# Expert blocks combined on TensorE: the last three of each layer instead of one, and VectorE-only adds of the rows read back

## The chip, the cores and the metric

The kernel runs on one core of a Trainium2 chip. The metric is the device time of one execution in microseconds. Before the change it is 2536.22 us, the median of three runs (2533.2 to 2540.05).

## The reference, cut to what matters

The program is one hybrid block followed by two decoder layers on 512 tokens of 1024 features. The change touches the mixture of experts that ends each decoder layer. Each token is given two of 32 experts; the reference sorts the 1024 assignments by expert, pads each expert's rows to blocks of 128, and computes

```
def expert_block(args):
    xe, e = args
    hid = jax.nn.silu(xe @ w_gate[e]) * (xe @ w_up[e])
    return hid @ w_down[e]

yb = lax.map(expert_block, (xb, block_expert)).reshape(-1, d)
y_assign = jnp.zeros((n_assign, d), yb.dtype).at[order].set(yb[slot])
y = jnp.einsum('tkd,tk->td', y_assign.reshape(n_tok, TOP_K, d), weights)
...
x = _layernorm(alpha * x + ffn, ln2_g[l], ln2_b[l])
```

Expert width is 256. What must come out is, for each token, the weighted sum of its two experts' rows, added to alpha times the residual and layer-normalised.

## The kernel before, in words

The residual `xr` stays on chip as four tiles of 128 tokens. In `layer_moe` (L1543 on) every layer does 18 blocks of 128 rows (`NB = 18`). Blocks 0 to 3 are one expert each; blocks 4 to 17 hold two experts each, a frequent one in rows 0 to 95 and a rare one in rows 96 to 127, whose numbers SyncE reads from a table at run time (`who_is`, L1832). An overflow path behind `tc.If(rv > 0)` (L1864 to L1916) serves rows that fit in no block.

For each block the loop (L1843 to L1862) issues the next block's weights on SyncE's queue (`load`, L1560 to L1579: for each expert 2 MB of gate and up and 1 MB of down), gathers the token rows of a later block with an indirect DMA on GpSimd's queue, and then calls

- `up` (L1765): 64 products on TensorE into a PSUM tile `gb`, SiLU on ScalarE, and a scale-and-multiply by the routing weight on VectorE into `es`, or `el` for the last block;
- `down` of the block before (L1774): two transposes, a copy to `hT` on ScalarE (L1780), 32 products into two PSUM tiles `db` (L1784);
- `scatter` of the block before (L1788): ScalarE and VectorE copy one half each to a tile `ey` (two buffers), and an indirect DMA on GpSimd's queue writes the rows into `yd` in DRAM, one place for each token and choice.

After the loop come, in program order: the readback of `yd` (`readback`, L1823: eight DMAs on SyncE's queue into four buffers `B`, each held until all scatters have landed); the load of the overflow count by every engine and the branch on it; the eight adds of the readback into `xr` (L1920), for each token tile one on VectorE and one on GpSimd; then `down`, `keep` and `combine` of block 17, whose rows go through no DRAM. `keep` (L1799) splits the block's output into a rounded part `y[:, 0]` (ScalarE) and the rest `y[:, 1]` (VectorE, L1802), and builds a 0/1 matrix `ST` from the token numbers. `combine` (L1807) multiplies `ST` with both parts on TensorE, for each token tile and half (two products, L1812), and VectorE adds the result to `xr`: fused with the sum that the layer norm needs if an `ln` is given (L1817), as a plain add otherwise (L1815, used only in the overflow path). The layer norm follows tile by tile.

The order of the work on each engine is set by a scheduler that simulates the program: an engine takes what is ready, earlier program text first. It doesn't move work across the branch. Buffers are named by pool: `big` has eight buffers `B`, `xH` and `xL` one each (seen as `XW` in the profile; they hold the gate and up weights of block 16), `wraw` has three buffers `R`, PSUM has two `gb`, three `db`, two `xb` and one `hb`.

Of the kernel before, what the change touches and what calls it, by code (L numbers as in the profile page):

```python
# [17 lines left out]
D = 1024  # L18
# [7 lines left out]
ALPHA = 4.0 ** 0.25  # L26
NP = (1, 1, 0, 0)
NS = 4
CAP = 96


# [1511 lines left out]
def layer_moe(k, l):  # L1543
# [37 lines left out]
    with ExitStack() as es:  # L1581
# [214 lines left out]
            tc.add_to_no_dep_group(f"rows{l}", n.ins)  # L1796
            puts.append(n.ins.name)

        def keep(pd, t0, t1, y, ST):  # L1799
            for h in range(2):  # L1800
                A.copy(y[:, 0, h], pd[h])
                V.tensor_sub(y[:, 1, h], pd[h], y[:, 0, h])  # L1802
            V.tensor_scalar(ST[:, 0:256], it, t0, None, op0=OP.is_equal)
            V.tensor_scalar(ST[:, 256:512], it, t1, None, op0=OP.is_equal)
            return ST, y

        def combine(ST, y, ln=None):  # L1807
            for t in range(4):
                for h in range(2):
                    p = gb()  # L1810
                    for b in range(2):
                        mm(p, ST[:, 128 * t:128 * t + 128], y[:, b, h], start=b == 0, stop=b == 1)  # L1812
                    x = xr[:, t, 512 * h:512 * h + 512]
                    if ln is None:
                        V.tensor_add(x, x, p)  # L1815
                    else:
                        V.scalar_tensor_tensor(x, x, 0.0, p, op0=OP.add, op1=OP.add, accum_out=ln.sums(t, h))  # L1817
                if ln:
                    ln.finish(t)
                    if l == 1:  # L1820
                        nc.sync.dma_start(k.out[128 * t:128 * t + 128], xr[:, t])

        def readback(t):  # L1823
            ya = k.big([2, D])
            for j in range(2):
                n = nc.sync.dma_start(ya[:, j], yd[T * j + 128 * t:T * j + 128 * t + 128])
                for put in puts:
                    tc.add_manual_dep(n.ins, put, mybir.DependencyInfo(mybir.DependencyClass.Sync, mybir.DependencyReason.DATA),
                                      reason="rows of every expert")
            return ya  # L1830
# [5 lines left out]
        def weights(b):  # L1836
            if b < NS:
                return [W[b] if b < 2 else load(b)]
            return [load(who_is(idi[0:1, b - NS, j:j + 1])) for j in range(2)]

        later, xT = None, [turned(xg[0])]
        ws = weights(0)
        for b in range(NB):  # L1843
            nxt = weights(b + 1) if b + 1 < NB else None
            if b == NB - 1:
                lgb = k.big([2, D])
                nc.sync.dma_start(lgb[:, 0], k.row(f"ln2_g{l}", 0, D))
                nc.sync.dma_start(lgb[:, 1], k.row(f"ln2_b{l}", 0, D))
            if b + 3 < NB:
                gather(xg[b % 3], xi[:, b + 3:b + 4])  # L1850
            h = up(ws, xT.pop(), tw[:, b:b + 1], rt([256], "el") if b == NB - 1 else half([256], "L", "es"))
            if later:
                pd = [db(), db()]
                down(later[1], later[0], pd)
                scatter(pd, b - 1)
            if b + 1 < NB:
                xT.append(turned(xg[(b + 1) % 3]))
            later = h, ws
            ws = nxt
            if 2 <= b < 6:  # L1860
                with tc.issue_after(k.gone.ins):
                    V.tensor_scalar(xr[:, b - 2], xr[:, b - 2], ALPHA, None, op0=OP.mult)  # L1862
        back = [readback(t) for t in range(4)]
        rv = nc.values_load(nx[0:1, 0:1], min_val=0, max_val=40)  # L1864
        with tc.If(rv > 0):
            turn, oh, o2, c1 = rt([1], "turn"), rt([32], "oh"), rt([32], "o2"), rt([8], "c1")
# [9 lines left out]
            with tc.For_i(0, rv, 1):  # L1876

                pr, r0, r1, tk, wa, t0_, t1_, zz = (c1[:, n:n + 1] for n in range(8))
                V.tensor_scalar(oh, cx, turn, None, op0=OP.is_le)
                V.reduce_sum(pr, oh, axis=AX)  # L1880
                V.tensor_scalar(oh, it[:, 0:32], pr, None, op0=OP.is_equal)
                V.tensor_tensor(o2, cx, ex, op=OP.subtract)
                V.tensor_tensor(o2, o2, oh, op=OP.mult)
                V.reduce_sum(r0, o2, axis=AX)
                V.tensor_sub(r0, turn, r0)
                pick(r1, cap)
                V.scalar_tensor_tensor(r0, r0, 128.0, r1, op0=OP.mult, op1=OP.add)
                V.tensor_copy(ci, pr)
                V.tensor_scalar(turn, turn, 1.0, None, op0=OP.add)
                for j in range(2):  # L1890
                    V.tensor_tensor(se, M[j], all4(oh), op=OP.mult)
                    V.reduce_sum(in_[j], se, axis=AX)
                    V.tensor_tensor(se, se, off, op=OP.mult)
                    V.reduce_sum(wx[j], se, axis=AX)
                    V.tensor_scalar(wx[j], wx[j], r0, None, op0=OP.subtract)
                    V.tensor_scalar(bad, wx[j], 0.0, None, op0=OP.is_lt)
                    V.tensor_sub(bad, bad, in_[j])
                    V.tensor_scalar(bad, bad, 1.0, 1000.0, op0=OP.add, op1=OP.mult)
                    V.tensor_add(wx[j], wx[j], bad)
                q = table()  # L1900
                pick(tk, q[:, 0:32])
                pick(wa, q[:, 32:64])
                tokens(tk, zz, t0_, t1_, None, gi)
                gather(xg[0], gi)
                pe = bass.ds(who_is(ci[0:1, 0:1]), 1)
                g, dn = weg[pe].rearrange("o p n -> (o p) n"), wed[pe].rearrange("o p n -> (o p) n")
                wu = []
                for u in range(2):
                    wu.append(k.big([4, 512]))
                    nc.sync.dma_start(wu[u], g[:, 2048 * u:2048 * u + 2048])  # L1910
                wd = k.wraw.tile([128, 4, 512], F32, name="R")
                nc.sync.dma_start(wd, dn)
                h = up([(wu, wd)], turned(xg[0]), wa, half([256], "L", "es"))
                pd2 = [db(), db()]
                down([(wu, wd)], h, pd2)
                combine(*keep(pd2, t0_, t1_, k.big([2, 2, 512], F32R), half([512], "H", "ST", F32R)))  # L1916

        for t in range(4):
            for j in range(2):
                (G if j else V).tensor_add(xr[:, t], xr[:, t], back[t][:, j])  # L1920
        pd = [db(), db()]
        down(later[1], later[0], pd)
        kept = keep(pd, t0[:, NB - 1:NB], t1[:, NB - 1:NB], k.big([2, 2, 512], F32R), half([512], "H", "ST", F32R))
        ln = LN(k, [lgb[:, 0, :512], lgb[:, 0, 512:]], [lgb[:, 1, :512], lgb[:, 1, 512:]], (1, 1, 1, 1), k.wsp.tile([128, 512], F32, name="ljunk", tag="H"))

        combine(*kept, ln)
# [44 lines left out]
```

## Time and profile before

| | us |
|---|---|
| median of 3 runs | 2536.22 |
| lowest, highest | 2533.2, 2540.05 |
| the profiled execution | 2534.45 |
| its span | 2532.7 |
| mean granted TensorE clock | 0.947 |

The profile holds one execution. All times in it count from the span's start. Its page says how long each engine was busy; the views used below group instructions by line (`L1920` is line 1920), give them in order of time, or sum up what each engine did in a stretch. "Idle before" is the time that an engine stood still ahead of an instruction, and the arrow names what ended it. Expert stages are the stretches in which the page's DMA row is at 9: layer 0's ends near 1620 us, layer 1's near 2481 us.

### The profile page before, as it was taken

The page shows a single profiled execution, that of the slowest core. Times are in us where ns is not written, and L with a number is a line of the kernel's source. Part 1 is how long each engine was busy: PE and PEld are TensorE (multiplying, and loading weights), DVE is VectorE, ACT ScalarE, POOL GpSimd, SP SyncE. Part 2 cuts the span into 40 slices and gives each one's busy share as a digit, 9 for nine tenths or more (in the row PEclk, how much of TensorE's full clock was granted, in tenths as well). Part 3 has the DMA queues.
Part 4 walks back from the last instruction along what each step waited for, and adds up shares of the span by engine and source line. Part 5 has one row for each costly group of instructions (what it writes and reads, how often), then busy time and mean ns, then how long its engine had stood idle before and what let it go on. Part 6 is the DMA issues. An engine that isn't in the chain of part 4 may idle for free. (4 is left out here: it accounts for less than half of the span.)

```text
span 2532.7 us, 33575 instructions
## 1 busy us (share of the span) xinstructions
PE 2291.8 (90%) x12992; PEld 1614.5 (64%) x12992; DVE 1170.5 (46%) x2412; ACT 810.1 (32%) x1670; POOL 518.1 (20%) x490
## 2 busy tenths in 40 slices
PE   6999899999999999999995988778999999788884
PEld 4888577888887777777783322267777677743221
DVE  3762677322336963454475211279444545721105
ACT  4373246333333343333331111144433333211112
POOL 2012342110101322012222210233110232211103
PEclk7999999999999999999997999889999999889997
DMA  6114522222234222121254999921222125369994
GB/s 247 67 53 145 186 84 84 84 99 93 100 109 177 98 75 84 50 84 60 85 205 162 360 405 402 376 76 67 75 71 74 44 75 208 110 239 403 398 410 192
DMA packets 71509, 406.12 MB, mean 160 GB/s; under 512 B 13561, under 2 KB 14233, under 8 KB 30256
## 3 DMA queue, kind: packets, MB, share of 16 engines
q1 hardware_dynamic: 55104, 368.09, 38.1%
q0 software_dynamic: 14032, 30.29, 3.6%
q10 hardware_dynamic: 2208, 5.54, 0.6%
q8 instruction: 104, 1.70, 0.3%
q14 instruction: 61, 0.50, 0.1%
HBM read 390.66 MB, written 32.51 MB: 167 GB/s over the span
## 5 line engine op out<-in xcount | busy, mean ns | idle before, releaser
L233 DVE TENSOR_TENSOR L<-R,H 128x512 fp32r<-128x512 f32 x417 | 302.3, 731 | 432.2 <-ACT H L232 424.9
L238 PE MATMUL bk<-xH,H 128*128 128x512 f32 (+2 forms) x1144 | 450.0, 396 | 1.9 <-DVE h L435 0.9
L239 PE MATMUL bk<-xL,H 128*128 128x512 f32 (+2 forms) x1144 | 451.7, 395 | 0.0
L240 PE MATMUL bk<-xH,L 128*128 128x512 f32 (+2 forms) x1144 | 448.2, 395 | 0.3 <-DVE L L233 0.3
L232 ACT CAST H<-R 128x512 fp32r<-128x512 f32 x447 | 274.1, 620 | 368.8 <-PE bk L239 265.1
L1770 PE MATMUL gb<-B,xT 128*32 128x512 f32 (+1 forms) x1152 | 229.9, 653 | 24.4 <-DMA B<-in_weg_dram 24.4
L240 PEld LDWEIGHTS bk<-xH,L 128*128 128x128 f32 (+1 forms) x1144 | 214.9, 188 | 52.4 <-issue 3.1
L239 PEld LDWEIGHTS bk<-xL,H 128*128 128x128 f32 (+1 forms) x1144 | 215.0, 188 | 47.6 <-issue 2.4
L238 PEld LDWEIGHTS bk<-xH,H 128*128 128x128 f32 (+1 forms) x1144 | 214.1, 188 | 48.6 <-PE bk L428 1.3
L239 PE MATMUL bk<-L,xH 128*128 128x256 f32 x640 | 184.1, 289 | 13.4 <-DVE L L233 13.4
L238 PE MATMUL bk<-H,xH 128*128 128x256 f32 x640 | 184.7, 290 | 3.8 <-ACT xH L1479 1.4
L240 PE MATMUL bk<-H,xL 128*128 128x256 f32 x640 | 181.9, 289 | 4.3 <-DVE xL L1480 4.3
L1770 PE MATMUL gb<-XW,xT 128*32 128x512 f32 (+1 forms) x768 | 144.2, 622 | 25.0 <-DMA XW<-in_weg_dram 25.0
L1770 PEld LDWEIGHTS gb<-B,xT 128*32 128x32 f32 (+1 forms) x1152 | 63.8, 125 | 137.3 <-issue 108.5
L239 PEld LDWEIGHTS bk<-L,xH 128*128 128x128 f32 x640 | 125.2, 196 | 14.8 <-DVE L L233 13.8
L238 PEld LDWEIGHTS bk<-H,xH 128*128 128x128 f32 x640 | 125.1, 196 | 6.5 <-ACT xH L1479 1.8
L240 PEld LDWEIGHTS bk<-H,xL 128*128 128x128 f32 x640 | 124.0, 196 | 6.1 <-DVE xL L1480 6.0
L1771 ACT ACTIVATE es<-gb 128x256 f32<-128x256 f32 x34 | 13.1, 384 | 344.3 <-PE gb L1770 344.3
L1446 POOL TENSOR_SCALAR e<-e,asm 128x128 f32<-128x128 f32 (+3 forms) x64 | 71.6, 1120 | 249.4 <-DVE asm L1445 195.5
L1784 PE MATMUL db<-R,hT 128*32 128x512 f32 (+1 forms) x576 | 105.8, 595 | 3.3 <-ACT hT L1780 2.5
L1244 DVE SCALAR_TENSOR_TENSOR B<-hp,cw,B 128x512 f32<-128x512 f32 x120 | 101.2, 870 | 1.5
L1792 POOL DMA_INDIRECT yd<-ey,ix x34 | 33.9, 997 | 314.1 <-DVE ey L1791 237.8
(626 smaller groups left out, 3862.6 us busy)
## 6 DMA issues: line engine op xcount, KB each, us to landing
B<-in_weg_dram SPq DMA_DIRECT2D x80, 1024.0 KB, 12.4
XW<-in_weg_dram SPq DMA_DIRECT2D x48, 1024.0 KB, 16.2
R<-in_wed_dram SPq DMA_DIRECT2D x40, 1024.0 KB, 11.5
R<-in_wgt_dram SPq DMA_DIRECT2D x32, 1024.0 KB, 4.8
R<-in_win_dram SPq DMA_DIRECT2D x31, 1024.0 KB, 7.5
R<-in_wmod_dram SPq DMA_DIRECT2D x24, 1024.0 KB, 4.8
B<-in_wed_dram SPq DMA_DIRECT2D x24, 1024.0 KB, 18.8
R<-in_wff_dram SPq DMA_DIRECT2D x22, 1024.0 KB, 5.0
```

Of the source, the lines that this page charges most:

```text
L232: nc.scalar.copy(H[:, :n], ap)
L233: (lo or nc.vector).tensor_sub(L[:, :n], ap, H[:, :n])
L238: mm(out, aH, bH, start=first, stop=False)
L239: mm(out, aH, bL, start=False, stop=False)
L240: mm(out, aL, bH, start=False, stop=last)
L1244: V.scalar_tensor_tensor(acc[:, f], src, w, acc[:, f], op0=OP.mult, op1=OP.add)
L1446: G.tensor_scalar(e[:, :N], e[:, :N], sm[:, h:h + 1], None, op0=OP.mult)
L1770: mm(pgu[r], xT[kt // 4][:, kt % 4, r], wu[kt // 4][:, kt % 4], start=kt == 0, stop=kt == 7)
L1771: A.activation(s, pgu[:, 0:256], AF.Silu)
L1784: mm(pd[n][r], hT[:, c, r], wd[:, 2 * n + c], start=c == 0, stop=c == 1)
L1792: n = G.indirect_dma_start(out=yd, out_offset=bass.IndirectOffsetOnAxis(ap=ix[:, b:b + 1], axis=0), in_=y, in_offset=None, bounds_check=2 ...
```

## The change

With `KEPT = 3` the blocks 15, 16 and 17 are all combined on TensorE, through a helper `put` that scatters a block below 15 and combines it otherwise; the combines of 15 and 16 use the plain add. `keep` now takes its two tiles from the pool of `ey`. The readback stands at the end of the iteration of block 16, behind `put(15)`; one of its four tiles is a buffer `B`, three are halves of `xH` and `xL`. Block 16 is put after the loop and ahead of the branch. Behind the branch come the adds, all on VectorE, and then `up`, `down`, `keep` and `combine` of block 17. The gather of a later block's rows is issued ahead of the two loads of layer-norm rows, which move from iteration 17 to 16.

```diff
--- before.py
+++ after.py
@@ -26,6 +26,7 @@
 ALPHA = 4.0 ** 0.25
 NP = (1, 1, 0, 0)
 NS = 4
+KEPT = 3
 CAP = 96
 
 
@@ -1796,10 +1797,12 @@
             tc.add_to_no_dep_group(f"rows{l}", n.ins)
             puts.append(n.ins.name)
 
-        def keep(pd, t0, t1, y, ST):
+        def keep(pd, t0, t1):
+            y = [ep.tile([128, 2, 512], F32R, name="yk", tag="ey") for b in range(2)]
+            ST = half([512], "H", "ST", F32R)
             for h in range(2):
-                A.copy(y[:, 0, h], pd[h])
-                V.tensor_sub(y[:, 1, h], pd[h], y[:, 0, h])
+                A.copy(y[0][:, h], pd[h])
+                V.tensor_sub(y[1][:, h], pd[h], y[0][:, h])
             V.tensor_scalar(ST[:, 0:256], it, t0, None, op0=OP.is_equal)
             V.tensor_scalar(ST[:, 256:512], it, t1, None, op0=OP.is_equal)
             return ST, y
@@ -1809,7 +1812,7 @@
                 for h in range(2):
                     p = gb()
                     for b in range(2):
-                        mm(p, ST[:, 128 * t:128 * t + 128], y[:, b, h], start=b == 0, stop=b == 1)
+                        mm(p, ST[:, 128 * t:128 * t + 128], y[b][:, h], start=b == 0, stop=b == 1)
                     x = xr[:, t, 512 * h:512 * h + 512]
                     if ln is None:
                         V.tensor_add(x, x, p)
@@ -1820,8 +1823,7 @@
                     if l == 1:
                         nc.sync.dma_start(k.out[128 * t:128 * t + 128], xr[:, t])
 
-        def readback(t):
-            ya = k.big([2, D])
+        def readback(t, ya):
             for j in range(2):
                 n = nc.sync.dma_start(ya[:, j], yd[T * j + 128 * t:T * j + 128 * t + 128])
                 for put in puts:
@@ -1838,29 +1840,41 @@
                 return [W[b] if b < 2 else load(b)]
             return [load(who_is(idi[0:1, b - NS, j:j + 1])) for j in range(2)]
 
-        later, xT = None, [turned(xg[0])]
+        later, xT, back = None, [turned(xg[0])], []
         ws = weights(0)
-        for b in range(NB):
-            nxt = weights(b + 1) if b + 1 < NB else None
-            if b == NB - 1:
+
+        def put(b, which):
+            pd = [db(), db()]
+            down(which[1], which[0], pd)
+            if b < NB - KEPT:
+                scatter(pd, b)
+            else:
+                combine(*keep(pd, t0[:, b:b + 1], t1[:, b:b + 1]))
+
+        for b in range(NB - 1):
+            nxt = weights(b + 1)
+            if b + 3 < NB:
+                gather(xg[b % 3], xi[:, b + 3:b + 4])
+            if b == NB - 2:
                 lgb = k.big([2, D])
                 nc.sync.dma_start(lgb[:, 0], k.row(f"ln2_g{l}", 0, D))
                 nc.sync.dma_start(lgb[:, 1], k.row(f"ln2_b{l}", 0, D))
-            if b + 3 < NB:
-                gather(xg[b % 3], xi[:, b + 3:b + 4])
-            h = up(ws, xT.pop(), tw[:, b:b + 1], rt([256], "el") if b == NB - 1 else half([256], "L", "es"))
+            h = up(ws, xT.pop(), tw[:, b:b + 1], half([256], "L", "es"))
             if later:
-                pd = [db(), db()]
-                down(later[1], later[0], pd)
-                scatter(pd, b - 1)
-            if b + 1 < NB:
-                xT.append(turned(xg[(b + 1) % 3]))
+                put(b - 1, later)
+            xT.append(turned(xg[(b + 1) % 3]))
             later = h, ws
             ws = nxt
             if 2 <= b < 6:
                 with tc.issue_after(k.gone.ins):
                     V.tensor_scalar(xr[:, b - 2], xr[:, b - 2], ALPHA, None, op0=OP.mult)
-        back = [readback(t) for t in range(4)]
+            if b == NB - 2:
+                homes = [k.big([2, D])]
+                for tag in ("xH", "xL"):
+                    t = k.xp.tile([128, 2, 4, 512], F32, name="XW", tag=tag)
+                    homes += [t[:, u].rearrange("p (j a) n -> p j (a n)", j=2) for u in range(2)]
+                back = [readback(t, homes[t]) for t in range(4)]
+        put(NB - 2, later)
         rv = nc.values_load(nx[0:1, 0:1], min_val=0, max_val=40)
         with tc.If(rv > 0):
             turn, oh, o2, c1 = rt([1], "turn"), rt([32], "oh"), rt([32], "o2"), rt([8], "c1")
@@ -1913,14 +1927,15 @@
                 h = up([(wu, wd)], turned(xg[0]), wa, half([256], "L", "es"))
                 pd2 = [db(), db()]
                 down([(wu, wd)], h, pd2)
-                combine(*keep(pd2, t0_, t1_, k.big([2, 2, 512], F32R), half([512], "H", "ST", F32R)))
+                combine(*keep(pd2, t0_, t1_))
 
         for t in range(4):
             for j in range(2):
-                (G if j else V).tensor_add(xr[:, t], xr[:, t], back[t][:, j])
+                V.tensor_add(xr[:, t], xr[:, t], back[t][:, j])
+        h = up(ws, xT.pop(), tw[:, NB - 1:NB], half([256], "L", "es"))
         pd = [db(), db()]
-        down(later[1], later[0], pd)
-        kept = keep(pd, t0[:, NB - 1:NB], t1[:, NB - 1:NB], k.big([2, 2, 512], F32R), half([512], "H", "ST", F32R))
+        down(ws, h, pd)
+        kept = keep(pd, t0[:, NB - 1:NB], t1[:, NB - 1:NB])
         ln = LN(k, [lgb[:, 0, :512], lgb[:, 0, 512:]], [lgb[:, 1, :512], lgb[:, 1, 512:]], (1, 1, 1, 1), k.wsp.tile([128, 512], F32, name="ljunk", tag="H"))
 
         combine(*kept, ln)
```

## Rows read from the trace of the kernel before

**Rows 1.** The page's busy row: engine, busy us, share of the span, instructions.
```profile
PE 2291.8 (90%) x12992; PEld 1614.5 (64%) x12992; DVE 1170.5 (46%) x2412; ACT 810.1 (32%) x1670; POOL 518.1 (20%) x490
```
**Rows 2.** Stretches: from:to, length, each engine's busy us, granted clock, DMA share, GB/s.
```profile
2463.00:2481.00 18.00, 17.10 (x134) 4.82 (x138) 1.17 (x2) 2.19 (x5) 1.04 (x2) 0.91 1.01 413
2481.00:2489.00 8.00, 6.90 (x62) 1.78 (x50) 1.17 (x2) 0.38 (x1) 0.98 (x1) 1.00 0.35 134
2494.00:2502.20 8.20, 1.29 (x3) 0.60 (x3) 4.47 (x3) 0.59 (x1) 5.88 (x3) 0.78 0.80 316
2502.20:2511.00 8.80, 6.66 (x14) 3.27 (x13) 7.85 (x27) 3.88 (x9) 3.28 (x2) 0.62 0.00 1
```
**Rows 3.** Timeline of TensorE, layer 1's tail: start, us, instruction, [idle before].
```profile
2463.44 8.75 PE L1770 MATMUL gb<-XW,xT 128*32 128x512 f32 x58 [2.49 <-DMA XW<-in_weg_dram]
...
2472.92 3.64 PE L1784 MATMUL db<-R,hT 128*32 128x512 f32 x32
2476.50 0.44 PE L1778 MATMUL hb<-ct,es 128*128 128x128 f32 x2
2477.39 3.64 PE L1784 MATMUL db<-B,hT 128*32 128x512 f32 x32 [0.46 <-ACT hT L1780]
2480.85 7.05 PE L1770 MATMUL gb<-B,xT 128*32 128x512 f32 x58
2489.47 0.41 PE L1778 MATMUL hb<-ct,el 128*128 128x128 f32 x2 [1.57 <-DVEq L1865]
2490.34 3.64 PE L1784 MATMUL db<-R,hT 128*32 128x512 f32 x32 [0.46 <-ACT hT L1780]
```
**Rows 4.** Waits of SyncE's queue, layer 1's tail: total us, times, longest.
```profile
SPq L1826 <- DMA yd<-ey,ix: 11.0, 1, 11.0
```
**Rows 5.** Timeline of VectorE, layer 1's tail.
```profile
2491.98 1.23 DVE L1920 TENSOR_TENSOR xr<-xr,B 128x1024 f32<-128x1024 f32 x1 [3.14 <-SPq L1865]
...
2498.28 2.39 DVE L1920 TENSOR_TENSOR xr<-xr,B 128x1024 f32<-128x1024 f32 x1 [1.11 <-DMA B<-yd]
2500.59 0.68 DVE L1802 TENSOR_TENSOR B<-db,B 128x512 fp32r<-128x512 f32 x1
...
2503.45 1.22 DVE L1920 TENSOR_TENSOR xr<-xr,B 128x1024 f32<-128x1024 f32 x1
2504.58 0.68 DVE L1817 SCALAR_TENSOR_TENSOR xr<-xr,gb 128x512 f32<-128x512 f32 x1
...
2509.45 0.68 DVE L1817 SCALAR_TENSOR_TENSOR xr<-xr,gb 128x512 f32<-128x512 f32 x1
...
2510.30 0.68 DVE L1817 SCALAR_TENSOR_TENSOR xr<-xr,gb 128x512 f32<-128x512 f32 x1
```
**Rows 6.** Timeline of layer 0's tail, several engines.
```profile
1610.64 0.63 PE L1770 MATMUL gb<-B,xT 128*32 128x512 f32 x3 [1.11 <-DMA B<-in_weg_dram]
...
1635.11 0.33 SPq L208 DMA_DIRECT2D R<-in_win_dram  x1
...
1643.46 0.67 DVE L1817 SCALAR_TENSOR_TENSOR xr<-xr,gb 128x512 f32<-128x512 f32 x1
...
1668.62 0.56 PE L238 MATMUL bk<-H,xH 128*128 128x256 f32 x1
```
**Rows 7.** Instructions by line, GpSimd, 2486 to 2512: count, busy us, mean ns, idle before.
```profile
L1920 POOL TENSOR_TENSOR xr<-xr,B 128x1024 f32<-128x1024 f32 x4 | 9.4, 2355 | 14.1 <-DVE ST L1804 10.2 <-DVE xr L1920 4.0
```
**Rows 8.** Timeline of ScalarE, layer 1's tail.
```profile
2487.94 0.38 ACT L1771 ACTIVATE el<-gb 128x256 f32<-128x256 f32 x1 [7.92 <-PE gb L1770]
...
2492.38 0.59 ACT L1801 CAST B<-db 128x512 fp32r<-128x512 f32 x1 [2.09 <-PE db L1784]
```
**Rows 9.** The branch's lines on VectorE's sequencer: ns min/median/max, first and last start.
```profile
L1864 DVEq TENSOR_LOAD <-nx x2: 307/310/314, 1626.9 to 2488.4; - x2
...
L1865 DVEq EVENT_SEMAPHORE  x2: 21/21/21, 1627.9 to 2489.3; - x2
```
**Rows 10.** Timeline of SyncE's queue, layer 1's tail.
```profile
2488.23 7.70 SPq L1826 DMA_DIRECT2D B<-yd  x8
```

## The prediction

> **What bounds the kernel now.** I read the page first, then each expert stage cut into stretches, then the engines' timelines through its tail, in both layers. TensorE is busy 90% of the span [rows 1], but the expert stage is bound by its weight stream: in 2463 to 2481 us the DMA engines are busy for the whole stretch at 413 GB/s, and only in 2481 to 2489 does their share fall to 0.35 [rows 2]. The tail of layer 1, which ends the kernel, starts there. Block 15 is the last but two, block 17 the last. TensorE waits 2.49 us for the weights of block 16, does its gate-and-up product from 2463.44, block 15's down product from 2472.92, block 16's from 2477.39 and block 17's gate-and-up from 2480.85 [rows 3]. Then the reader should see the path leave TensorE: SyncE waits 11.0 us for the scattered rows to land [rows 4], VectorE's first readback add starts at 2491.98, its third ends at 2500.67, and only then comes the subtraction that block 17's combine needs, although the down product that feeds it ended at 2493.98 [rows 3, 5]. From the second fused add of the combine (2504.58) on, VectorE is the bound: 7.85 us busy of 8.8 in 2502.2 to 2511 [rows 2, 5]. Layer 0 has the same pattern 861.4 us earlier; there that second fused add is at 1643.46 [rows 6].
>
> I therefore follow one instant through the change: when that second fused add starts. All of the layer norm hangs behind it, and in layer 0 the next layer's first products (1668.62) too [rows 6].
>
> **What goes.** Two scatters per layer (blocks 15 and 16), with their ScalarE and VectorE copies, and with them the 11.0 us wait [rows 4]; readback now needs block 14's rows only. The four adds on GpSimd go: they take 2.36 us each [rows 7]. VectorE's own take 1.23 us and up to 2.39 while one of those runs [rows 5]; all eight on VectorE are 8 x 1.23 = 9.8 us. The add after the first fused add (1.22) leaves the middle of the combine [rows 5].
>
> **What comes, layer 1, on the clock of before.** Up to 2472.92 nothing changes: block 15's scatter is replaced behind its down product, not ahead of it.
> - Down of 15: 3.64, to 2476.6 [rows 3].
> - Combine of 15: 16 products, eight adds. In 2502.2 to 2511, 14 such products kept TensorE busy 6.66 us at a granted clock of 0.62 [rows 2]; 16 at full clock are an estimated 16 x 0.48 x 0.62 = 4.7. TensorE also has block 16's transposes (0.44) and down product (3.64), which can fill its waits [rows 3]: 8.8 together, to 2485.4. The adds run alongside: two neighbouring fused adds without a visible wait are 0.85 apart (2509.45 and 2510.30) [rows 5], so eight take 6.8 and end at about the same time. A plain add has not been seen here; it is bounded by the bare 0.68 of the fused one and by that 0.85, and I take 0.85, because two PSUM banks are handed back and forth as there.
> - Block 16's two halves use the two buffers which block 15's combine reads, so they wait for it. Cast 0.59, subtraction 0.68 and an estimated 0.8 of products and handover [rows 5, 8]: first add at 2487.5. Eight adds: 2494.3. Behind this wait on VectorE stand the branch and the readback adds.
> - The branch on the overflow count: on VectorE 0.9 us from the load of the count (2488.4) to its last semaphore (2489.3) [rows 9]. To 2495.2. TensorE follows: before, its first product behind the branch waited for VectorE's semaphore as well [rows 3].
> - Gate-and-up of 17, moved from ahead of the branch to behind it. 58 of its 64 products took 7.05 at clock 1.00, and block 16's 58 took 8.75 in a stretch at 0.91 [rows 2, 3]. I take 7.5: to 2502.7.
> - SiLU, scale, transpose, copy: 2487.94 to 2490.34 before, 2.4, with about 0.5 of branch in it [rows 3, 8]; 1.9, to 2504.6. Down 3.64: 2508.2. Cast, subtraction, first fused add and handover, 0.59 + 0.68 + 0.68 + 0.35 = 2.3: the second fused add at **2510.5**, 5.9 later than 2504.58.
> - The six fused adds after it took 2504.58 to 2510.30, 0.95 each; with no GpSimd add to wait for I give them 0.85: 0.6 back. Layer 1: **+5.3**.
>
> Layer 0 is the same less 861.4. It gets two more small credits: today block 15's down product stands behind products of block 17 that wait 1.11 us for weights at 1610.64 [rows 6]; those move away, so it starts some 0.8 earlier. And its second fused add came 0.3 later than layer 1's. 5.9 - 0.8 - 0.3 - 0.6 = **+4.2**.
>
> **Costed at nothing.** The readback adds: 9.8 us behind the branch lie beside gate-and-up, its chain and down of 17 (13.0 us). If that cover were short, each microsecond is one on the path. The readbacks: SyncE can issue them from about 2477, behind the last weight load; before, the third add's data were there 10 us after the first issue (2488.23, 2498.28) [rows 5, 10], so they land at about 2487, 8 us ahead of need. Nothing else is queued behind them but the branch. In layer 0 the next layer's first weight load (1635.11) waits for a buffer that block 17's down product frees, now about 11 us later; its user runs at 1668.62 [rows 6], so some 20 us of cover remain. The LayerNorm rows and the gather that change places are issued ahead of need in both kernels.
>
> **The sum.** +5.3 + 4.2 = +9.5 on the profiled execution (2534.45: span 2532.70 and 1.75 around it) gives 2544.0. The median shown is 1.77 above that execution: **2545.7**, said as 2546.
>
> **Rivals.**
> 1. *No visible change.* If adds follow each other at their bare 0.68, 16 x 0.17 = 2.7 comes off per layer, and 0.45 more if gate-and-up takes 7.05: +9.5 - 6.3 = +3, 2539; somewhat less if the next layer's start absorbs part. For it: nothing else runs on VectorE at that time. Against: the pitch of 0.85 and more in every row at hand.
> 2. *The clock falls.* In 2494 to 2502.2 TensorE was busy 1.29 us of 8.2 and the granted clock was 0.78, and 0.62 after it [rows 2]: it goes to 1.2 GHz after little work. The second combine has TensorE about half busy, and the branch stops it. Gate-and-up at the lower level would be 14.1 instead of 7.5, +6.6 per layer: 2552 with one layer, 2559 with both. Against: clock 1.00 in 2481 to 2489, just behind a 0.46 us wait. The Trainium skill (TensorE: Matmul & The Clock Gate, "What's actually happening") says that the half rate is the default and activity releases it; that speaks for this rival as soon as the combine leaves the engine idle enough, and no stretch of this trace is busy to just that degree.
> 3. *Faster.* Both combines hide beside the weight stream, where VectorE is busy only 1.17 us of 18 [rows 2]. Then gate-and-up of 17 starts at 2480.85 + 0.9 for the branch, and the second fused add at 2481.8 + 7.05 + 1.9 + 3.64 + 2.3 = 2496.7: -7.9, and -8.2 in layer 0: 2520. It decides at VectorE's branch: a layer gains if this is done before 2495.2 - 5.3 = 2489.9. For it: the 11.0 us wait and the late subtraction are really gone, and an order in which block 15's down product runs within the 2.49 us wait at 2461 would start everything some 10 us earlier. Against: in the trace that product starts at 2472.92, 8 us before the weights are all there, and two combines in series need 16.
> 4. *The adds don't hide* (the change doesn't do what it says): the readbacks land late or the SiLU's scale waits behind adds on VectorE, 1 to 2 us per layer. This is inside the forecast's range.
>
> **Chances.** Forecast (2539 to 2553, with 4): 0.50. Rival 1: 0.20. Rival 2: 0.13. Rival 3: 0.17. A measurement here can tell about 0.3%, 7.6 us, from no change. Faster by more than that: rival 3, 0.17. Within: rival 1 and the 0.16 of the forecast that lies below 2543.8, 0.36. Slower: the rest of the forecast, 0.34, and rival 2, 0.47. The range 2526 to 2558 leaves out most of rival 3 and the slowest of rival 2, under 0.2.
>
> **What would show it.** Right: no wait of SyncE for scattered rows; all readback adds behind the branch, about 1.2 us each, done before block 17's down product; in layer 1 eight plain adds from about 2477.8 and eight from 2487.5; gate-and-up of 17 starting near 2495 instead of 2481; the second fused add near 2510, and in layer 0 near 1648. Wrong: a first down product of the three well before 2472; the branch passed on VectorE before 2490; a granted clock near one half under gate-and-up of 17; adds of the first combine ending later than 2487.

## The result and the profile after

The changed kernel takes 2554.79 us (median of 4 runs, 2553.92 to 2555.97) where the kernel before takes 2534.71 in the same comparison: ratio 1.0077, 95% interval 1.0064 to 1.0089, so 16 to 23 us slower. The forecast was slower by 9.5. The sign held, and so did the wide range (2526 to 2558); the forecast's own band (2539 to 2553) was missed by 1.8 us. The size is half of what was measured, and the runs below show which term is missing.

In the views PE is TensorE, PEld its weight loads, DVE VectorE, ACT ScalarE, POOL GpSimd and SPq SyncE's queue; DVEq is VectorE's sequencer, which runs the branch. TensorE's timeline through layer 1's tail after the change (start and duration in us, instruction, idle time before it and what ended it), to be read against [rows 3]:

```profile
2472.07 8.75 PE L1771 MATMUL gb<-XW,xT 128*32 128x512 f32 x58 [2.50 <-DMA XW<-in_weg_dram]
2481.56 3.64 PE L1785 MATMUL db<-R,hT 128*32 128x512 f32 x32 [0.74 <-ACT hT L1781]
...
2485.33 1.11 PE L1815 MATMUL gb<-yk,ST 128*128 128x512 f32 x2
2486.37 1.92 PE L1785 MATMUL db<-B,hT 128*32 128x512 f32 x16
...
2488.64 1.92 PE L1785 MATMUL db<-B,hT 128*32 128x512 f32 x16
...
2503.81 7.07 PE L1771 MATMUL gb<-B,xT 128*32 128x512 f32 x64 [1.25 <-DVEq L1879]
2513.86 0.69 PE L1779 MATMUL hb<-ct,es 128*128 128x128 f32 x2 [2.97 <-DVE es L1773]
2515.05 6.10 PE L1785 MATMUL db<-R,hT 128*32 128x512 f32 x32 [0.51 <-ACT hT L1781]
```

Block 16's gate-and-up stands at 2472.07, block 15's down product at 2481.56, and block 17's gate-and-up has gone behind the branch, to 2503.81. Then comes what the forecast did not have: TensorE idles 2.97 us for the scale of the SiLU (L1773), and block 17's down product takes 6.10 us (in layer 0 2.98 and 6.02). The same 32 products took 3.64 before [rows 3].

VectorE's timeline of the same stretch shows why, to be read against [rows 5]:

```profile
2488.75 0.69 DVE L1818 TENSOR_TENSOR xr<-xr,gb 128x512 f32<-128x512 f32 x1 [2.15 <-PE gb L1815]
2491.04 1.28 DVE L1818 TENSOR_TENSOR xr<-xr,gb 128x512 f32<-128x512 f32 x2 [1.60 <-PE gb L1815]
...
2495.58 0.69 DVE L1818 TENSOR_TENSOR xr<-xr,gb 128x512 f32<-128x512 f32 x1 [0.23 <-PE gb L1815]
2496.18 1.28 DVE L1805 TENSOR_TENSOR yk<-db,yk 128x512 fp32r<-128x512 f32 x2
2497.46 1.28 DVE L1818 TENSOR_TENSOR xr<-xr,gb 128x512 f32<-128x512 f32 x2
...
2501.99 1.29 DVE L1818 TENSOR_TENSOR xr<-xr,gb 128x512 f32<-128x512 f32 x2 [0.23 <-PE gb L1815]
2503.72 1.23 DVE L1934 TENSOR_TENSOR xr<-xr,B 128x1024 f32<-128x1024 f32 x1 [0.43 <-DVEq L1879]
...
2509.93 3.48 DVE L1934 TENSOR_TENSOR xr<-xr,XW 128x1024 f32<-128x1024 f32 x3
2513.33 0.47 DVE L1773 SCALAR_TENSOR_TENSOR es<-es,tw,gb 128x256 f32<-128x256 f32 x1
...
2523.38 0.69 DVE L1820 SCALAR_TENSOR_TENSOR xr<-xr,gb 128x512 f32<-128x512 f32 x1 [0.23 <-PE gb L1815]
```

Eight adds of block 15's combine, two subtractions, eight adds of block 16's, the branch, then the eight readback adds (L1934) without a gap, with only two short steps for block 17's selection matrix among them (0.52 us), and only behind the last of them, at 2513.33, the scale. Gate-and-up had ended at 2503.81 + 7.07 = 2510.88. The Trainium skill (TensorE: Matmul & The Clock Gate, the table at its head) calls VectorE's queue strictly first in, first out; the trace agrees, the scale passes no add.

Stretches of the same tail (from:to, length, busy us of PE, PEld, DVE, ACT and POOL, granted clock, DMA share, GB/s):

```profile
2489.00:2503.80 14.80, 11.80 (x45) 4.78 (x38) 11.41 (x19) 1.07 (x2) 0.00 (x0) 1.00 0.84 334
2503.80:2511.00 7.20, 7.07 (x64) 2.36 (x64) 7.20 (x8) 0.06 (x1) 0.00 (x0) 1.00 0.02 6
2511.00:2514.00 3.00, 0.14 (x1) 0.14 (x2) 2.80 (x4) 0.33 (x1) 0.00 (x0) 0.87 0.00 0
2515.00:2521.20 6.20, 6.15 (x33) 1.43 (x34) 0.69 (x1) 0.58 (x1) 0.00 (x0) 0.59 0.00 0
```

The clock stays at 1.00 through both combines and gate-and-up, starts to fall in the idle stretch and is 0.59 on average under the down product. Cut into single microseconds it is 0.50, the lower of its two levels (1.2 GHz), from 2514 to 2520, and 0.97 in the one after.

SyncE's queue in the tail (start, us, instruction, count), against the 11.0 us wait of [rows 4]:

```profile
2485.25 0.34 SPq L1559 DMA_DIRECT2D R<-in_wed_dram  x1
2485.89 0.80 SPq L1828 DMA_DIRECT2D B<-yd  x2
2486.74 9.14 SPq L1828 DMA_DIRECT2D XW<-yd  x6
```

The readbacks follow the last weight load at once; that wait is gone, as the change intends.

Counted from the start of block 15's down product, the second fused add comes at 41.82 us in layer 1 (31.66 before, [rows 3, 5]) and at 41.72 in layer 0 (1607.93 to 1649.65; 32.78 before). Before, the down product of layer 0 starts at the following line of TensorE's timeline, in between gate-and-up products; its second fused add is in [rows 6].

```profile
1610.68 0.62 PE L1784 MATMUL db<-R,hT 128*32 128x512 f32 x1
```

### The profile page after: what moved, and what is told of

The parts are those of the page before. It is cut to its first block, busy times and chain, and to the rows that moved or that the text cites. A ratio compares the mean times of both kernels' runs of the same rounds, so it can differ in the third digit from the quotient of the medians.

```text
span 2551.9 us, 33728 instructions
## 1 busy us (share of the span) xinstructions
PE 2310.2 (91%) x13052; PEld 1619.5 (63%) x13056; DVE 1198.5 (47%) x2464; ACT 811.5 (32%) x1674; POOL 495.1 (19%) x478
## 5 line engine op out<-in xcount | busy, mean ns | idle before, releaser
L1757 DVE COPY xT<-xb 128x512 f32<-128x512 f32 x36 | 24.9, 691 | 152.3 <-PE gb L1771 109.4
## 6 DMA issues: line engine op xcount, KB each, us to landing
B<-in_weg_dram SPq DMA_DIRECT2D x80, 1024.0 KB, 14.1
```

What stands on the lines that cost most here:

```text
L1757: (A.copy if h else V.tensor_copy)(xT, p.rearrange("p (c t) -> p c t", c=4))
```

## Experiments

Theory: two combines in series, with gate-and-up of 17 behind the branch, cost about what was forecast, and the other half is the scale queued behind the readback adds, counted twice: as a wait, and as the clock that TensorE loses in it. Rivals: longer combines; a slow down product for a reason of its own; a combine that costs its time wherever it stands.

The diffs are cut to the lines that matter and go against the changed kernel (7 and 8: the kernel before); their comments behind # were added here. Ratios are against the kernel before in the same comparison; "tail" is the time from the start of block 15's down product to the second fused add, layer 1, profiled execution.

| run | median us | ratio, 95% interval | tail us |
|---|---|---|---|
| after | 2554.8 | 1.0077 [1.0064, 1.0089] | 41.8 |
| 1 scale first | 2545.7 | 1.0043 [1.0028, 1.0058] | 37.2 |
| 2 fill the gap | 2552.1 | 1.0069 [1.0056, 1.0082] | 39.1 |
| 3 two blocks | 2552.0 | 1.0071 [1.0058, 1.0084] | 39.3 |
| 4 two, up early | 2542.2 | 1.0035 [1.0022, 1.0048] | 35.4 |
| 5 no first combine | 2541.9 | 1.0026 [1.0016, 1.0035] | 35.2 |
| 6 two, own buffers | 2540.4 | 1.0019 [1.0010, 1.0028] | 30.7 |
| 7 before, VectorE only | 2535.8 | 1.0004 [0.9995, 1.0013] | 29.8 |
| 8 before, subtractions first | 2534.4 | 0.9997 [0.9988, 1.0006] | 27.2 |
| 9 as 5, adds split | 2529.2 | 0.9980 [0.9971, 0.9989] | 30.7 |
| 10 up between | 2552.7 | 1.0070 [1.0056, 1.0084] | 40.2 |
| 11 four blocks | 2549.5 | 1.0053 [1.0039, 1.0067] | 36.6 |
| 12 two, mended | 2534.6 | 0.9997 [0.9987, 1.0007] | 30.5 |

(before: tail 31.7. Where the order of the adds after the second fused one differs, as in 6 to 8, the tail alone does not give the end.)

**1. The scale put forward.**

```diff
+        h = up(ws, xT.pop(), tw[:, NB - 1:NB], half([256], "L", "es"))
-        for t in range(4):
+        for t in range(3):
             for j in range(2):
                 V.tensor_add(xr[:, t], xr[:, t], back[t][:, j])
-        h = up(ws, xT.pop(), tw[:, NB - 1:NB], half([256], "L", "es"))
+        with tc.issue_after(k.gone.ins):    # k.gone: the scale
+            for j in range(2):
+                V.tensor_add(xr[:, 3], xr[:, 3], back[3][:, j])
```

> The scale of block 17's SiLU is put on VectorE behind six of the eight readback adds instead of behind all eight; nothing else is changed. Theory (the excess over the forecast is this wait, and the clock that TensorE loses in it): the scale runs at the end of gate-and-up plus the SiLU, some 2.0 us earlier, TensorE's gap before the transposes falls from 3.0 to about 1 us, and down of 17 takes 3.7 us instead of 6.1; about 4.4 us per layer, 2546 in all. If only the wait counts and the clock falls anyway: 4 us in all, 2551. If the excess lies elsewhere (longer combines, the stage before): 2555, as after the change.

Measured 2545.7, 9.1 below the changed kernel. TensorE's timeline of this run, layer 1:

```profile
2503.62 7.07 PE L1771 MATMUL gb<-B,xT 128*32 128x512 f32 x64 [1.25 <-DVEq L1879]
2511.70 0.44 PE L1779 MATMUL hb<-ct,es 128*128 128x128 f32 x2 [1.01 <-DVE es L1773]
2512.65 3.64 PE L1785 MATMUL db<-R,hT 128*32 128x512 f32 x32 [0.51 <-ACT hT L1781]
```

The gap falls from 2.97 to 1.01, the down product is back at 3.64, and the tail is shorter by 4.7 us (4.6 in layer 0). Nearly half of the loss hung on where one instruction of 0.47 us stood in VectorE's queue.

**2. Wait kept, gap filled.**

```diff
...
+                    last = mm(pgu[r], xT[kt // 4][:, kt % 4, r], wu[kt // 4][:, kt % 4], start=kt == 0, stop=kt == 7)
+            if fill:                        # 28, in block 17's gate-and-up alone
+                with tc.issue_after(last.ins):
+                    p = xb()
+                    for f in range(fill):
+                        c = f % 4
+                        nc.tensor.transpose(p[:, 128 * c:128 * c + 128], xg[0][:, 128 * c:128 * c + 128], ident)
```

> The scale still waits behind all eight adds, but TensorE gets 28 transposes of a tile that nobody reads, behind block 17's gate-and-up, so that it does not idle while it waits (work added, none left out). Theory with the clock as a cause of its own: the transposes for down of 17 start no earlier, but down takes 3.7 us instead of 6.1: some 2.4 us less per layer, 2550. Rival (down of 17 is slow for another cause, such as its weights or the adds on VectorE): down stays at 6.1, the time at 2555 or a little above.

TensorE's timeline of this run, layer 1:

```profile
2504.55 7.07 PE L1771 MATMUL gb<-B,xT 128*32 128x512 f32 x64 [1.26 <-DVEq L1885]
2511.55 3.28 PE L1777 MATMUL xb<-ct,xg 128*128 128x128 f32 x28
2514.67 0.38 PE L1785 MATMUL hb<-ct,es 128*128 128x128 f32 x2
2515.56 3.64 PE L1791 MATMUL db<-R,hT 128*32 128x512 f32 x32 [0.51 <-ACT hT L1787]
```

The adds still hold the scale (2514.07 here), yet the down product takes 3.64, at a granted clock of 1.00 where it was 0.59: its 6.10 was the clock and nothing else. The tail is 2.7 us shorter in layer 1 and 2.6 in layer 0. The median fell by only 2.7 in all where two tails give 5.3; the two intervals leave room for that (1.0077 and 1.0069, each uncertain by 0.0013), so the tails, not the median, carry this size. So of the 4.7 us of the first run about 2.6 is clock and 2.1 the wait itself.

**3 and 4. Two blocks instead of three.** Run 3 sets KEPT to 2. Run 4 also moves gate-and-up of 17 ahead of the branch:

```diff
+        h = up(ws, xT.pop(), tw[:, NB - 1:NB], rt([256], "el"))
         put(NB - 2, later)
         rv = nc.values_load(nx[0:1, 0:1], min_val=0, max_val=40)
```

In run 4 block 17's down product reads the tile of the overflow branch instead of the one that its gate-and-up wrote; the work is the same, but block 17's own rows are left out of the sum.

> The last two blocks instead of three are combined (KEPT = 2): block 15 is scattered again. Theory (the two combines in series stand on the path, gate-and-up of 17 behind them): one combine's 8.7 us per layer leave the path, but the readbacks now wait for block 15's scatter, land around 2503 on the clock after the change, so the adds end near 2506 instead of 2513: 7 us per layer less, 2540 (2537 to 2543). Rival (the cost is that gate-and-up of 17 and the adds went behind the branch, and the combine of 15 hides beside the weights): 2552 or more.

> As the kernel with two blocks combined, and gate-and-up of block 17 with its scale is written ahead of the branch again, in front of block 16's combine. Theory: gate-and-up (7 us) lies beside the weights and the scattered rows' landing, the branch passes VectorE near 2491 on the clock before the change, the readback adds run from about 2492 to 2502 and the second fused add comes near 2503: 1 to 2 us per layer before that of the kernel before, 2531. Rival (the order of gate-and-up does not count): as the kernel with two blocks combined, 2540.

Both missed, by 12 and 11 us. VectorE's timeline of run 3, layer 1:

```profile
2493.69 1.29 DVE L1805 TENSOR_TENSOR yk<-db,yk 128x512 fp32r<-128x512 f32 x2 [7.33 <-DMA yd<-ey,ix]
2495.27 1.29 DVE L1818 TENSOR_TENSOR xr<-xr,gb 128x512 f32<-128x512 f32 x2 [0.29 <-PE gb L1815]
```

VectorE idles 7.33 us ahead of the first subtraction of block 16's combine, at first beside block 16's down product (to 2490.04) and then for a scatter's DMA: the cast rows lie in the two buffers of the scatters (tag ey), and one of them still holds the rows that block 15's scatter reads. Block 16's first add comes 13.3 us behind the start of block 15's down product; in run 5 below, without the first combine and without this wait, it comes 9.0 behind it. The wait took the place of a combine, so run 3 says nothing on what a combine costs.

Run 3 also shows that a gap does not always cost the clock. TensorE's timeline, layer 0:

```profile
1641.48 0.44 PE L1779 MATMUL hb<-ct,es 128*128 128x128 f32 x2 [2.98 <-DVE es L1773]
1642.42 3.64 PE L1785 MATMUL db<-R,hT 128*32 128x512 f32 x32 [0.51 <-ACT hT L1781]
```

The gap is as long as after the change and stands behind the same gate-and-up of 7.07 us, yet the clock stays at 1.00 and the down product takes 3.64. In its layer 1 the gap is 2.97 and the down product takes 5.34.

In run 4 the same waiting falls beside gate-and-up, but there all eight readback adds and the subtractions share VectorE behind the branch: the tail is 3.7 us over that of before in layer 1 and 2.7 in layer 0 (35.5 against 32.8), 6.4 of the 7.7 measured.

**5 and 9. Without the first combine**, on run 1.

```diff
-                combine(*keep(pd, t0[:, b:b + 1], t1[:, b:b + 1]))
+                kept = keep(pd, t0[:, b:b + 1], t1[:, b:b + 1])
+                if b > NB - KEPT:
+                    combine(*kept)
```

> On top of the kernel with the scale put forward (first experiment, 2545.7): block 15's down product, casts and selection matrix stay, but the 16 products and eight adds of its combine are left out in both layers, so its rows never reach the sum. Theory (the two combines stand in series on the path, as the prediction had it): block 16's down product no longer runs between them and block 16's first add comes at about 2490.8 instead of 2497.25 in layer 1; everything behind it moves by the same 6.5 us; both layers 13 us, 2533. Rival (the first combine hides beside the weight stream, and what is left of the loss lies in the order of gate-and-up and the branch): 2543 to 2546.

Measured 2541.9: the interval (2540 to 2545) takes in the rival's 2543 and leaves out the theory's 2533. The trace shows where the theory's gain went. TensorE's and VectorE's timelines, layer 1, in two fences:

```profile
2496.30 7.07 PE L1771 MATMUL gb<-B,xT 128*32 128x512 f32 x64 [1.03 <-DVEq L1881]
2505.61 0.69 PE L1779 MATMUL hb<-ct,es 128*128 128x128 f32 x2 [2.24 <-DVE es L1773]
2506.80 6.38 PE L1785 MATMUL db<-R,hT 128*32 128x512 f32 x32 [0.51 <-ACT hT L1781]
```

```profile
2498.06 1.23 DVE L1937 TENSOR_TENSOR xr<-xr,XW 128x1024 f32<-128x1024 f32 x1 [0.63 <-SPq L1881]
...
2500.53 1.23 DVE L1937 TENSOR_TENSOR xr<-xr,XW 128x1024 f32<-128x1024 f32 x1 [0.72 <-DMA XW<-yd]
...
2505.08 0.47 DVE L1773 SCALAR_TENSOR_TENSOR es<-es,tw,gb 128x256 f32<-128x256 f32 x1
```

Gate-and-up did come 6.2 us earlier (16.06 us behind block 15's down product, 22.26 in run 1): the first combine is on the path. But adds that start earlier wait for rows still landing, the scale again stands behind six of them, and gap and clock are back. Run 9 therefore leaves four adds ahead of the scale and puts four behind it (`range(2)` and `range(2, 4)` in the diff of run 1):

> As the experiment without block 15's combine (its rows never reach the sum), but only four readback adds stand ahead of the scale of block 17's SiLU and four behind it. There, 4.2 of the 6.2 us that gate-and-up won were given back at the scale, because adds that came earlier had to wait for rows still on their way. Theory: with four adds ahead the scale is not held, down of 17 keeps 3.64 us, and the whole 6.2 us per layer are won against the first experiment (2545.7): 2533.3. Rival (what was given back hangs on the landing of the rows by itself): as before, 2541.9.

Measured 2529.2. TensorE's timeline of run 9, layer 1:

```profile
2484.05 7.07 PE L1771 MATMUL gb<-B,xT 128*32 128x512 f32 x64 [1.03 <-DVEq L1881]
2492.13 0.44 PE L1779 MATMUL hb<-ct,es 128*128 128x128 f32 x2 [1.01 <-DVE es L1773]
2493.07 3.64 PE L1785 MATMUL db<-R,hT 128*32 128x512 f32 x32 [0.51 <-ACT hT L1781]
```

VectorE idles 1.79 us ahead of the scale, the down product has 3.64 again, and the tail is 30.7 us, 6.5 below run 1 (31.3 and 5.8 below in layer 0), in line with the theory. The median is 4 us lower still than the two tails explain. In the profiled executions 5.0 us of the difference lie between the tails, from layer 1's first product to its block 15's down product (809.2 us in run 1, 804.2 here), where the two kernels are the same; the cause is open.

**6. Two blocks with buffers of their own.**

```diff
-        def keep(pd, t0, t1):
+        def keep(pd, t0, t1, free=None):        # free = xg[:2] for block 16
...
+            y = [free[b].rearrange("p (j a) -> p j a", j=2).bitcast(F32R) if free else ep.tile([128, 2, 512], F32R, name="yk", tag="ey") for b in range(2)]
...
+        h17 = up(ws, xT.pop(), tw[:, NB - 1:NB], rt([256], "el"))
         put(NB - 2, later)
...
+                (G if j else V).tensor_add(xr[:, t], xr[:, t], back[t][:, j])
```

> Two blocks combined (KEPT = 2), gate-and-up of block 17 ahead of the branch, the cast rows of block 16 kept in the two gathered tiles that are free by then instead of in the scatter's buffers, and each second readback add on GpSimd as before. Theory: no subtraction waits for a scatter any more; VectorE passes the branch near 2495 on the clock before the change, held by gate-and-up and eight adds, down of 17 runs behind it, and the second fused add comes near 2504, as in the kernel before (2504.6): 2534, within 3 us. Rival (a second combine costs its 7 us wherever it stands): 2545 or more.

Measured 2540.4, between the two. The second fused add is where the theory put it (tail 30.7), but in layer 1 the last one comes 38.9 us behind block 15's down product (2474.97 to 2513.89), before 37.4 [rows 3, 5], because readback adds now stand between the fused adds; in layer 0 it is 41.3 against 38.6, with a down product of 17 that takes 5.34 us. But the next layer's first product, which waits for layer 0's end, starts only 0.4 us later (58.3 us behind the same start, before 57.9 [rows 6]). So some 2 of the 4.5 us are placed; the rest is open. A second combine does not cost 7 us wherever it stands.

**7 and 8. The kernel before with one part changed.** Run 7 replaces `(G if j else V)` by `V`. Run 8 moves two row tiles' adds into the combine:

```diff
+                        if t < 2 and h == 1:
+                            with tc.issue_after(f.ins):   # f: this fused add
+                                add(t + 2)
```

> The kernel before with one part of the change alone: all eight readback adds on VectorE. Theory (in the kernel before, these adds wait for rows that land late, so four more on VectorE fill its waits): the second fused add stays within 1 us of 2504.6; 2535. Rival (putting the adds on one engine is itself a loss of four adds of 1.22 us per layer, less the contention with GpSimd): 2540.

> The kernel before with another order alone: the readback adds of the third and fourth row tile are put behind the first fused adds (behind the second fused add of tile 0 and of tile 1), so that the subtraction for block 17's combine no longer stands behind the third add. Theory (VectorE's order is the bound there): first fused add near 2499 instead of 2502.2, but the same work is left behind it; 1 to 2 us per layer, 2531. Rival (landing of the rows sets the end): 2534.5.

Run 7: no difference (1.0004). Giving GpSimd's four adds to VectorE costs nothing where VectorE was waiting for rows anyway; the second fused add comes 1.9 us earlier in its tail, which is more than the 1 us allowed for, and the last one 0.7 earlier (36.7). Run 8: no difference (0.9997), where 3 us were expected; the interval just reaches that far. VectorE's timeline of run 8, layer 1:

```profile
2500.81 0.69 DVE L1817 SCALAR_TENSOR_TENSOR xr<-xr,gb 128x512 f32<-128x512 f32 x1 [0.29 <-PE gb L1812]
...
2503.90 2.89 DVE L1923 TENSOR_TENSOR xr<-xr,B 128x1024 f32<-128x1024 f32 x1
...
2511.26 0.68 DVE L1817 SCALAR_TENSOR_TENSOR xr<-xr,gb 128x512 f32<-128x512 f32 x1
```

The second fused add comes 4.5 us earlier in its tail (27.2 against 31.7), the last one at 37.6 as before (37.4): an add that moves behind the fused adds is paid for there, one of them with 2.89 us.

**10. Gate-and-up between the combines**, three blocks, gate-and-up of 17 ahead of block 16's down product as in run 4 (with its own tile).

> Three blocks combined as after the change, but gate-and-up of block 17 with its scale is written ahead of the branch, in front of block 16's down product. On TensorE it then runs between the products of the two combines. Theory (the combines' adds on VectorE are the chain, and block 16's products wait behind gate-and-up on TensorE): block 16's combine moves back by about what gate-and-up moved forward, the readback adds then stand between the branch and the subtraction; second fused add near 2523, as after the change: 2555. Rival (gate-and-up behind the branch is itself the loss): 7 us per layer less, 2541.

Measured 2552.7, as the theory had it. TensorE's timeline, layer 1:

```profile
2494.63 7.07 PE L1771 MATMUL gb<-B,xT 128*32 128x512 f32 x64
2501.63 0.73 PE L1815 MATMUL gb<-yk,ST 128*128 128x512 f32 x2
...
2509.14 0.41 PE L1779 MATMUL hb<-ct,el 128*128 128x128 f32 x2 [1.15 <-DVEq L1880]
2510.01 5.14 PE L1785 MATMUL db<-R,hT 128*32 128x512 f32 x32 [0.46 <-ACT hT L1781]
```

Gate-and-up starts 8.3 us earlier in the tail (13.9 against 22.25), block 16's products wait behind it, and the down product starts only 4.2 us earlier; the subtractions then stand behind readback adds. That gate-and-up went behind the branch is therefore not itself the loss: the combines and adds on VectorE make the chain with it in either place.

**11. Four blocks** (KEPT = 4 on run 1).

> The kernel with the scale put forward (first experiment, 2545.7) with four blocks combined (KEPT = 4): block 14's scatter is replaced as well. Its 16 products stand ahead of block 16's gate-and-up on TensorE, where that waits 2.5 us for weights. Theory (a combine hides only as far as such a wait reaches): block 16's gate-and-up starts some 5 us later but then finds all its weights (7.05 us instead of 8.75); 3.3 us per layer, 2552. If it is serial in full: 8.7 us per layer, 2563. If it hides beside the weight stream: 2546.

```profile
2473.22 1.33 PE L1815 MATMUL gb<-yk,ST 128*128 128x512 f32 x4 [0.19 <-DVE xr L1818]
2474.74 7.07 PE L1771 MATMUL gb<-XW,xT 128*32 128x512 f32 x64 [0.19 <-DVE xr L1818]
```

Measured 2549.5, between hiding in full (2546) and the theory (2552). In the lines above, of TensorE in layer 1, block 16's gate-and-up starts behind block 14's combine and runs in 7.07 instead of 8.75: most of that combine hides in the wait for weights. It costs (2549.5 - 2545.7) / 2 = 1.9 us per layer by the medians. The two intervals overlap and leave room for nothing as for some 4 us, but not for the 6.5 that block 15's costs in layer 1.

**12. Two blocks, mended:** run 9's order of adds, KEPT = 2, block 16's cast rows in the two free gathered tiles, nothing left out.

> Complete again: two blocks combined (KEPT = 2), block 15 scattered, gate-and-up of block 17 behind the branch as after the change, the cast rows of block 16 in the two gathered tiles that are free, all adds on VectorE, four ahead of the scale of block 17's SiLU and four behind it. It differs from the run with one combine and split adds (2529.2) only in that block 15's rows are scattered, so that the readbacks wait for them (about 11.7 us behind the start of block 15's down product, in the third experiment) and the first data come when the branch is passed, about 16 us behind that start. Theory: the adds are met just in time, 2530, within 3 us; faster than the kernel before by 3 to 5 us. Rival (the adds come late and the scale or the subtractions wait for them): 2537 or more, as the other kernels with two blocks.

Measured 2534.6, ratio 0.9997: level with the kernel before, not 4 us under it. In layer 1 the adds are met nearly in time. VectorE's timeline there:

```profile
2489.54 1.23 DVE L1939 TENSOR_TENSOR xr<-xr,B 128x1024 f32<-128x1024 f32 x1 [1.35 <-DMA B<-yd]
...
2494.14 0.48 DVE L1773 SCALAR_TENSOR_TENSOR es<-es,tw,gb 128x256 f32<-128x256 f32 x1 [0.83 <-ACT es L1772]
2494.54 4.77 DVE L1939 TENSOR_TENSOR xr<-xr,XW 128x1024 f32<-128x1024 f32 x4
```

One wait of 1.35 us for rows, none at the scale but that for the SiLU, and the down product takes 3.64. In layer 0 they are not met in time: VectorE waits 2.87 us for rows, the scale stands behind adds again, and TensorE idles 1.89 us for it, though the down product keeps 3.64. The last fused add comes 35.6 us behind block 15's down product in layer 1 and 37.1 in layer 0 (before: 37.4 and 38.6), 3.4 us earlier in sum, of which what follows the last fused add takes 0.8 back (23.2 us to the end, before 22.4). That fits the profiled execution, 2.8 us shorter than the one before (2531.61 against 2534.45), but the median of eleven executions lies 3.0 above it, and the interval (0.9987 to 1.0007) leaves room for no gain as for 3 us. The expectation also counted on the 4 us by which run 9 lies below its tails. No complete version here is shown to beat the kernel before.

## Why the prediction was right in sign and half in size

In steps of layer 1, from the start of block 15's down product (forecast; measured):

- First add of block 16's combine: 14.6; 15.9. Block 16's down product came in two halves among block 15's combine, which delayed it.
- End of its eight adds: 21.4; 21.7. They follow each other by 0.755 (1.28 for two and 0.23 of wait), not by the 0.85 taken. The two errors cancel, which is luck. Nor was the 0.85 what it was taken for: between the two adds that it was read from [rows 5], VectorE reads out a sum and runs three short instructions of the layer norm (2510.05 to 2510.30).
- Gate-and-up of 17: 22.3 for 7.5 us; 22.25 for 7.07. The clock was 1.00, so rival 2 fell where it was placed: TensorE was busy for 11.80 of 14.80 us in the combines (2489 to 2503.8) and not for half. That 2554.8 lies among the times named for it (2552 and 2559) is chance; the clock fell later, under the down product, behind a wait that rival 2 does not have.
- Start of down of 17: 31.7; 33.5. Its length: 3.64; 6.10.
- Second fused add: 37.6; 41.8.

One of the signs of being wrong came true by a little: the adds of the first combine ended 14.7 us behind the start of block 15's down product, where 14.1 had been set. And one of the signs of being right was met for the wrong reason: the readback adds were done before block 17's down product because that product had to wait for them.

**The step that failed** is the one headed "costed at nothing": "The readback adds: 9.8 us behind the branch lie beside gate-and-up, its chain and down of 17 (13.0 us)." The sum of lengths was right, the order was not. VectorE has one queue, and an instruction of that chain, the scale, stands in it behind the last add; only gate-and-up and the SiLU, 7.07 + 0.4, are cover for adds that stand ahead of it, and those take 9.6. Rival 4 named this wait at 1 to 2 us per layer; it was 2.1. Nothing in the forecast had what follows from it: TensorE idles 2.97 us, and the next 32 products take another 2.5 at the lower clock. The page of the Trainium skill cited above (section "HAM oscillation — how this bites in real kernels") says that a long enough wait between bursts of products throttles the engine again and the next burst starts slow. The trace of the changed kernel agrees, 0.59 behind the gap in layer 1 and 0.60 in layer 0; behind as long a gap, layer 0 of run 3 has 1.00. Wait and clock make 4.6 us per layer, 9.2 of the 20.1.

The rest stands as forecast: with the scale put forward the change costs 1.0043 [1.0028, 1.0058], 7 to 15 us, against the forecast 9.5. That it is the combines in series which cost this is shown by run 9 (one of them out: 6.5 and 5.8 us of tail), and that most of a combine can hide where TensorE waits for weights by run 11. The wait for scattered rows which the change removes was real, but VectorE had room in it: four more adds there cost nothing (run 7). Rival 3 needed block 15's down product early; it stayed 9.5 us behind block 16's gate-and-up, in both kernels.

## What to carry to other kernels

Work is hidden beside another engine only if no link of that engine's chain has to pass through the same queue behind it: list the queue's order, not the sum of its durations. A wait that leaves TensorE idle is to be priced for itself and, as a risk, once more for the products behind it at the lower clock: that came in both layers of the changed kernel, and in one of two in run 3. When blocks are taken out of a scatter, look at which buffers they then share with the scatters that remain.

## What the runs showed of the hardware that was not expected

- Neither the length of a gap nor the products ahead of it tell whether TensorE's clock falls. Behind 7.07 us of gate-and-up at full clock, an idle 1.01 us left the down product at 3.64 us (run 1, both layers), 2.97 brought 6.10 (after), and 2.98 left it at 3.64 in layer 0 of run 3. Ahead of the branch, 1.57 us left 3.64 before the change [rows 3] and brought 5.34 in layer 1 of runs 7 and 8, behind the same products. In run 10 1.15 us brought 5.14 in layer 1 and 1.14 left 3.64 in layer 0. What decides was not found. TensorE's timeline of run 7, layer 1:

```profile
2493.62 0.41 PE L1778 MATMUL hb<-ct,el 128*128 128x128 f32 x2 [1.57 <-DVEq L1865]
2494.49 5.34 PE L1784 MATMUL db<-R,hT 128*32 128x512 f32 x32 [0.46 <-ACT hT L1780]
```

- The clock can fall when the gap is already over: in run 7 it is 1.00 until 2495 and 0.50 to 0.52 from there to 2498, while the products run from 2494.49 on.
- Single executions of one kernel wander by some microseconds (run 12: 2528.8 to 2539.1 over 11 runs), and part of it lies ahead of the stage that was changed: block 15's down product of layer 0 starts at 1607.93 after the change and at 1610.27 in run 1, where nothing ahead of it differs. Another part lies between the tails (run 9). So effects of 2 us per layer are read in the tails of the traces; the medians confirm only their sums.
